# Two queues for the first loads, six cast buffers, and two row tiles transposed in float16

## The chip, the cores and the metric

The kernel runs on one core of a Trainium2 chip. The time is in device microseconds (us) for one execution of the whole program. Before the change three runs took 305.96, 309.68 and 311.07 us, so the median is 309.68. The run that was profiled took 306.58 us, and its profile spans 304.8 us from the first to the last instruction.

The engines have short names in the profile: PE is TensorE (matmuls; PEld are its weight loads), DVE is VectorE, ACT is ScalarE, POOL is GpSimd, SP is SyncE. Each works through its own instructions in order. A letter q behind a name (SPq) means the sequencer of that engine, which issues DMAs.

## The reference

```python
def setup_inputs():
    batch, m, k, n = 16, 512, 1024, 768
    return {
        "x": np.random.randn(batch, m, k).astype(np.float32),
        "w1": np.random.randn(k, n).astype(np.float32),
        "w2": np.random.randn(k, n).astype(np.float32),
    }

def reference(x: np.ndarray, w1: np.ndarray, w2: np.ndarray) -> np.ndarray:
    y1 = np.matmul(x, w1)
    y2 = np.matmul(x, w2)
    return (np.tanh(y1) * y2).astype(np.float32)
```

All inputs and the output are float32. There are 16 x 512 = 8192 rows of x with 1024 columns, and two weights of 1024 x 768.

## The kernel before

**Tiling.** The rows of x are cut into 64 row tiles of 128 rows (`mt`, 0 to 63). The contraction of 1024 is cut into eight slices of 128 (`k`). A weight slice a0 to a7 is 128 rows of w1, b0 to b7 of w2. The 768 output columns are cut into 512 (`F`) and 256 (`G`). All products are float16 with float32 sums. TensorE needs x with its contraction on the partitions, so every row tile is transposed first; the result is called `xT`.

**Three stages.** The first six row tiles, the head, are multiplied plainly: eight slices for each output, at L434. Row tiles 6 to 62 are 19 triples. For a triple, a fast matrix multiplication scheme is used: sums of x blocks (`S`, on VectorE, L419) are multiplied with sums of weight blocks (`B`, L409) in 15 products of four matmuls with 512 columns each (L462), and the products are combined with copies on ScalarE (L468) and additions on VectorE (L477). In this way 60 matmuls do the work of 72. Row tile 63 is plain again. Each output tile is a tanh on ScalarE (L440, L480) and a multiplication on VectorE (L444, L485), and is then stored by SyncE (L428).

**How x and the weights come in.** In the head, SyncE alone loads float32 data: row tiles 0 to 3 (`x0` to `x3`, 512 KB each, L332, into tiles called `x_f`) and the 16 weight slices (384 KB each, L336, into `w_f`), in the order of the list `loads` (L520): x0 a0 x1 a1 x2 a2 x3 a3 a4 and so on up to b7. Twelve buffers hold weight slices, so the last four wait until a slice has been cast to float16 (`cast_w`, L344; the copy itself is L340 on ScalarE or L342 on VectorE). Row tiles 0 to 3 are transposed on TensorE in float32, in two halves of four 128x128 blocks each (`transpose_pe`, L349), and each half is copied from PSUM to `xT` as float16 (`evacuate`).

From row tile 4 on, GpSimd issues a DMA that casts to float16 while loading (`load_x`, L369, into `xh`). Row tiles 4 and 5 are transposed on TensorE in float16 (`transpose_pe_h`, L359; eight blocks go into one bank). All later ones are transposed by a DMA that SyncE issues (L372).

**Buffers.** The cast tiles `xh` of row tiles 6 and up rotate through three buffers. Row tiles 4 and 5 have two buffers of their own, which are then not used again. A load into a buffer (`load_x`) waits until the transpose of the row tile that used it has landed (`T`), and until ScalarE has summed that tile's absolute values (`D`, L375). That sum, taken for every row tile and weight slice, feeds a test at the end of the kernel: if a magnitude is out of range, a slower general path would run. `xT` has four sets of three buffers.

**What sets the order.** A planner in the file (`Planner`, L78) simulates all operations with costs and due times, and its result is the order in which instructions are emitted on each engine, and the choice between ScalarE and VectorE where both are possible. It models DMA as one stream: `bandwidth` (L138) is the time at which the stream is free, `xfer` a transfer's length and `latency` the time to landing. The order of the products in a triple is written by hand (`PE_ORDER`, L75). While the first loads run, TensorE performs `WARM` matmuls of 256 columns on constant data (L724); nothing uses their results.

Of the kernel before, what the change touches and what calls it, by code (L numbers as in the profile page):

```python
# [77 lines left out]
class Planner:  # L78
# [13 lines left out]
    def op(self, name, engines, due, needs, fn, *args, behind=(), issued=(), chains=(), xfer=0.0, latency=None, seeds=False):  # L92


        assert name not in self.ops, name
        self.ops[name] = dict(engines=engines, due=due, needs=[n for n in needs if n], behind=[n for n in behind if n], issued=[n for n in issued if n], fn=fn, args=args,
                              chains=chains, xfer=xfer, latency=latency, seeds=seeds)
        for c in chains:
            self.chains.setdefault(c, {"left": 0, "bank": None, "end": 0.0})["left"] += 1
# [35 lines left out]
    def run(self, soon):  # L135
        free = {"none": 0.0, "pe": 0.0, "act": 0.0, "dve": 0.0, "pool": 0.0, "sp": 0.0}
        port = {"dve": 0.0, "pool": 0.0}
        bandwidth = 1.75  # L138
        left = {n: len(o["needs"] + o["behind"] + o["issued"]) for n, o in self.ops.items()}
        ready_at, end, engine_of, start_of = dict.fromkeys(self.ops, 0.0), {}, {}, {}  # L140
        ready = {e: [] for e in free}
# [10 lines left out]
        while len(end) < len(self.ops):  # L152
            best = None
            for e, names in ready.items():
# [20 lines left out]
                s, due, n = min((o for o in options if o[0] <= first + 0.02), key=lambda o: o[1])  # L175
                ahead = max(0.4, self.LOOK * self.ops[n]["engines"][e])
                urgent = [o for o in options if o[0] < first + ahead and o[1] + lag < min(due + lag, o[0] + 1.0)]
                if urgent and e != "pe":
                    s, due, n = min(urgent, key=lambda o: o[1])
# [6 lines left out]
            s, e, n = best  # L186
# [8 lines left out]
            f = s + o["engines"][e]  # L195
# [3 lines left out]
            if o["xfer"]:  # L199
                bandwidth = max(bandwidth, f) + o["xfer"]  # L200
# [32 lines left out]
def kernel(  # L233
# [17 lines left out]
    nc = tc.nc  # L251
    P = 128
    B, M, K = x.shape
    _, N = w1.shape
    KO = K // P
    KH = KO // 2
    MT = B * M // P
# [3 lines left out]
    TAIL = 1  # L261
    TRIPLES = (MT - HEAD - TAIL) // 3
    LOW, HIGH = 512.0, 1024.0
    XH_BUFS, XT_BUFS, S_BUFS, O_BUFS, C_BUFS, WF_BUFS = 3, 4, 2, 3, 2, 12
    WARM = 12
    SOON = {"S": 3.0, "D": 3.0}
    STORED = 5
    GATE = 2
    POOL_FROM = 99
    BY_PE = 6  # L270
    FILL = (-10, -6, -4, -2)
    bf16, f16, f32, i32 = mybir.dt.bfloat16, mybir.dt.float16, mybir.dt.float32, mybir.dt.int32

    xf = x.flatten_outer_dims().rearrange("(mt p) k -> mt p k", p=P)
# [8 lines left out]
    xhpool = pool("xh", 1)  # L283
# [16 lines left out]

    head_stack = ExitStack()
    wfpool = head_stack.enter_context(tc.tile_pool(name="wf", bufs=WF_BUFS))
    xfpool = head_stack.enter_context(tc.tile_pool(name="xf", bufs=4))
    steady = {}

    pin = tc.keep_in_program_order
# [1 line left out]
    plan = Planner(8)  # L308
    op = plan.op
# [6 lines left out]
    xfs, wfs, xhs, xts, ss, cs, os_ = {}, {}, {}, {}, {}, {}, {}  # L316
# [3 lines left out]
    def home(pool, key, shape, dtype):  # L320

        if (pool.name, key) not in fixed:
            fixed[pool.name, key] = pool.tile(shape, dtype, name=key)
        return fixed[pool.name, key]
# [3 lines left out]
        return xts[mt]  # L328

    def load_xf(e, mt):  # L330
        xfs[mt] = xfpool.tile([P, K], f32, tag="xf", name="x_f")
        pin(nc.sync.dma_start(xfs[mt], xf[mt]))  # L332

    def load_w(e, t, k, queue):
# [3 lines left out]
    def copy(e, dst, src):  # L338
        if e == "act":
            pin(nc.scalar.copy(dst, src))  # L340
        else:
            pin(engine[e].tensor_copy(dst, src))  # L342

    def cast_w(e, t, k):  # L344
        copy(e, wh[:, k, t * N:(t + 1) * N], wfs[t, k])

    def transpose_pe(e, mt, h, chain):
        for k in range(KH):
# [12 lines left out]
    def evacuate_h(e, mt, chain):  # L361
        copy(e, x_t(mt).rearrange("p k m -> p (k m)"), bank(chain).bitcast(f16))

    def xh_slot(mt):
        return XH_BUFS + mt - 4 if mt < BY_PE else (mt - BY_PE) % XH_BUFS

    def load_x(e, mt):
        xhs[mt] = home(xhpool, f"xh{xh_slot(mt)}", [P, K], f16)
        pin(nc.gpsimd.dma_start(xhs[mt], xf[mt]))  # L369

    def transpose(e, mt):
# [148 lines left out]
    plan.strict = [f"{p}.{i}" for _, i, p in sorted(sequence)]  # L520

    loads = "x0 a0 x1 a1 x2 a2 x3 a3 a4 a5 a6 a7 b0 b1 b2 b3 b4 b5 b6 b7".split()
    slices = [("ab"[t], t, k) for t in range(2) for k in range(KO)]
    for n, what in enumerate(loads):
        i = int(what[1])
        xfer = 1.3 if what[0] == "x" else 1.02
        before = f"L{loads[n - 1]}" if n else ""
        if what[0] == "x":
            op(f"L{what}", {"sp": 0.05}, 0.1 * n - 100, [], load_xf, i, issued=[before], xfer=xfer, latency=0.6)
        else:  # L530
            t = "ab".index(what[0])
            j = t * KO + i - WF_BUFS
            op(f"L{what}", {"sp": 0.05}, 0.1 * n - 100, [], load_w, t, i, nc.sync,
               issued=[before], behind=[f"c{slices[j][0]}{slices[j][2]}" if j >= 0 else ""], xfer=xfer, latency=0.6)
    for a, t, k in slices:
        op(f"c{a}{k}", {"dve": 0.5, "act": 0.74}, 6 + 1.3 * k + 9.5 * t,
           [f"L{a}{k}"], cast_w, t, k)
        op(f"aw{a}{k}", {"act": 0.92}, 80 + 10 * (t * KO + k), [f"c{a}{k}"], abs_w, t, k)
    for mt in range(4):
        for h in range(2):  # L540
            due = 5 + 2.3 * mt + 0.1 * h
            op(f"PT{mt}{h}", {"pe": 0.45}, due, [f"Lx{mt}"], transpose_pe, mt, h, ("T", mt, h), chains=[("T", mt, h)])
            op(f"e{mt}{h}", {"dve": 0.6, "act": 0.5}, due + 0.5, [f"PT{mt}{h}"] + ([f"e{mt}0"] if h else []), evacuate, mt, h,
               ("T", mt, h), chains=[("T", mt, h)])
        op(f"D{mt}", {"act": 1.05}, 30 + mt, [f"PT{mt}1"], abs_x, mt)

    PRODUCERS = {mt: [f"e{mt}0", f"e{mt}1"] if mt < 4 else [f"T{mt}"] for mt in range(MT)}
    xt_readers = {mt: [] for mt in range(MT)}

    def plain(mt, t, which, chain, due, at=0, first=True, behind=()):  # L550
        for k in range(KO):
            needs = ([f"cb{k}"] if t or which == "M" else []) + ([f"ca{k}"] if not t or which == "M" else [])
            needs.append(f"e{mt}{k // KH}" if mt < 4 else f"T{mt}")
            if not first and k == 0:
                needs.append(f"m{mt - 1}{t}{which}0")
            before = list(behind) + ([f"m{mt}{t}{which}0"] if k else [])
            n = G if which == "G" else F
            rhs = wh[:, k, t * N + (F if n == G else 0):t * N + F + (G if n == G else 0)]
            if which == "M":
                rhs = wh[:, k, :].rearrange("p (t n) -> p t n", t=2)[:, :, F:]  # L560
            op(f"m{mt}{t}{which}{k}", {"pe": MG if n == G else MM}, due(k), needs, mm, chain, slice(at, at + n), mt, k,
               rhs, first and k == 0, behind=before, chains=[chain])
        last = [f"m{mt}{t}{which}{k}" for k in range(KO)]
        xt_readers[mt] += last
        return last
# [25 lines left out]
    for mt in list(range(4, HEAD)) + list(range(MT - TAIL, MT)):  # L591
# [6 lines left out]
        for n, (t, which) in enumerate(parts):  # L598
            last = plain(mt, t, which, (which, mt, t), lambda k: base + 1.7 * n + 0.2 * k,
                         behind=[plan.strict[FILL[n]]] if tail else ())  # L600
# [23 lines left out]
    for v, a, b, how in B_SUMS:  # L624
        needs = []
# [22 lines left out]
    for i in range(TRIPLES):  # L648
        for v, a, b, how in A_SUMS:
            op(f"S{v}.{i}", {"pool": 1.12} if v in ON_POOL and i >= POOL_FROM else {"dve": 0.34}, None, x_needs(i, a) + x_needs(i, b), x_sum, i, v, a, b, how,  # L650
               behind=[f"{r}.{i - S_BUFS}" for r in a_readers[v]] if i >= S_BUFS else [])
# [3 lines left out]
        for o in C_OPS:  # L655
            name, kind, needs = o[:3]
            needs = [f"{n}.{i}" for n in needs]
            chains = sorted({(i, p) for p in o[3:6] if isinstance(p, str) and p[0] == "c"})
# [9 lines left out]
            if kind in ("seed", "copy", "add"):  # L668
                before = []
                if o[3][0] == "s":  # L670
                    before = [f"{r}.{i - C_BUFS}" for r in readers[o[3]]] if i >= C_BUFS else ["pools"]
# [6 lines left out]
            mt = HEAD + 3 * i + r  # L678
            due = soonest[name] + LAST + slot_of[i, "p10"]
            if kind in ("t", "th"):  # L680
                lo, n = (0, F) if kind == "t" else (F, G)
                op(f"{name}.{i}", {"act": 0.5 if n == F else 0.29}, due, needs, c_tanh, i, r, o[4], lo, n, o[5],
                   behind=reuse_out(mt), chains=chains)
            else:
                lo, n, at = (0, F, 0) if kind == "m" else (F, G, G)
# [9 lines left out]
    for mt in range(MT - TAIL - 3):  # L695
        op(f"st{mt}", {"sp": 0.05}, 40 + 4.33 * mt if mt >= HEAD else 110 + 13 * mt, outs[mt], store, mt,
           issued=[f"T{HEAD + 3 * (STORED + mt)}"] if mt < HEAD else [], xfer=1.1)
    for mt in range(4, MT):
        j = mt - XH_BUFS
        prev = f"L{mt - 1}" if mt > 4 else "gate"  # L700
        op(f"L{mt}", {"pool": 0.55}, None, [], load_x, mt,
           issued=[prev], behind=[f"T{j}", f"D{j}"] if j >= BY_PE else [], xfer=1.5)
        if mt < BY_PE:
            op(f"PT{mt}", {"pe": 0.5}, None, [f"L{mt}"], transpose_pe_h, mt, ("T", mt), chains=[("T", mt)])
            op(f"T{mt}", {"dve": 0.67, "act": 0.93}, None, [f"PT{mt}"], evacuate_h, mt, ("T", mt), chains=[("T", mt)])
            plan.ops[f"PT{mt}"]["due"] = 26 + 4 * (mt - 4)
        else:
            op(f"T{mt}", {"sp": 1.35}, None, [f"L{mt}"], transpose, mt,
               issued=[f"T{mt - 1}"] if mt > BY_PE else [],
               behind=xt_readers[mt - 3 * XT_BUFS] if mt >= 3 * XT_BUFS else [], xfer=1.45, latency=2.2)  # L710
        op(f"D{mt}", {"act": 1.05}, ORIGIN - 12 + 4.33 * (mt - HEAD), [f"L{mt}"], abs_x, mt)
# [8 lines left out]
    order = plan.run(SOON)  # L720
# [3 lines left out]
        pin(nc.tensor.matmul(banks[n % 8][:, n // 8 % 2 * 2 * P:][:, :2 * P], ones.bitcast(bf16)[:, :P], ones.bitcast(bf16), start=True, stop=True))  # L724
    make_identity(nc, ident)
    pin(nc.vector.tensor_copy(ident_h, ident))
    for n in sorted(order, key=lambda n: plan.start_of[n]):
        o = plan.ops[n]
        o["fn"](plan.engine_of[n], *o["args"])
    fast.close()  # L730
# [100 lines left out]
```

## Time and profile before

| | us |
|---|---|
| median of three runs (lowest, highest) | 309.68 (305.96, 311.07) |
| profiled run; span of its profile | 306.58; 304.8 |
| TensorE busy | 294.0 (96%) |
| VectorE busy | 239.8 (79%) |
| ScalarE busy | 221.2 (73%) |
| GpSimd busy | 33.0 (11%) |

The profile has several views, and the prediction uses these. The page gives busy times and 40 slices of the span; in the rows of slices each digit is a share in tenths, and PEclk is the clock that TensorE was granted. A table by stage gives the busy time of PE, PEld, DVE, ACT and POOL in a stretch, with the number of instructions in brackets, then the granted clock, the share of time in which the 16 DMA engines had a packet in work, and GB/s. The timeline lists instructions by start and length; in square brackets stands how long the engine was idle before, and which engine and tile ended that. The list of waits adds these up: engine, line, what it waited for, us in total, times, longest. Matmuls are pipelined, and the length drawn for one (0.379 us for 512 columns) is longer than the distance from one start to the next; a gap of TensorE is therefore longer than it looks.

### The profile page before, as it was taken

The page shows a single profiled execution, that of the slowest core. Times are in us where ns is not written, and L with a number is a line of the kernel's source. Part 1 is how long each engine was busy: PE and PEld are TensorE (multiplying, and loading weights), DVE is VectorE, ACT ScalarE, POOL GpSimd, SP SyncE. Part 2 cuts the span into 40 slices and gives each one's busy share as a digit, 9 for nine tenths or more (in the row PEclk, how much of TensorE's full clock was granted, in tenths as well). Part 3 has the DMA queues.
Part 4 walks back from the last instruction along what each step waited for, and adds up shares of the span by engine and source line. Part 5 has one row for each costly group of instructions (what it writes and reads, how often), then busy time and mean ns, then how long its engine had stood idle before and what let it go on. Part 6 is the DMA issues. An engine that isn't in the chain of part 4 may idle for free. (4 is left out here: it accounts for less than half of the span.)

```text
span 304.8 us, 4455 instructions
## 1 busy us (share of the span) xinstructions
PE 294.0 (96%) x1409; PEld 138.7 (45%) x1409; DVE 239.8 (79%) x497; ACT 221.2 (73%) x438; POOL 33.0 (11%) x67
## 2 busy tenths in 40 slices
PE   6999999999999799999999999999999999999994
PEld 4665544444444344444444444444444444444442
DVE  1217999888969597878988889797978989789754
ACT  4598978989885758687586866858686777775641
POOL 0030111110201011011020201111011101100000
PEclk9799999999999999999999999999999999999999
DMA  7999989999999999999999999999999999992143
GB/s 242 412 399 219 163 135 133 149 157 280 169 204 281 162 262 242 211 257 243 253 219 235 243 207 187 235 212 205 251 187 208 178 239 226 170 260 103 69 175 123
DMA packets 82585, 64.80 MB, mean 213 GB/s; under 512 B 63616, under 2 KB 64128, under 8 KB 82560
## 3 DMA queue, kind: packets, MB, share of 16 engines
q1 hardware_dynamic: 73920, 48.77, 66.0%
q0 software_dynamic: 8640, 15.73, 34.6%
q8 instruction: 11, 0.18, 0.2%
q14 instruction: 14, 0.11, 0.2%
HBM read 39.85 MB, written 25.17 MB: 213 GB/s over the span
## 5 line engine op out<-in xcount | busy, mean ns | idle before, releaser
L462 PE MATMUL bank<-b,s 128*128 128x512 f16 x608 | 141.0, 379 | 0.3 <-DVE bank L477 0.3
L462 PEld LDWEIGHTS <-s 128*128 128x128 f16 x760 | 74.4, 98 | 90.1 <-issue 0.6
L477 DVE TENSOR_TENSOR bank<-bank,s 128x512 f32<-128x512 f32 x95 | 65.8, 694 | 27.0 <-ACT s L468 17.6
L468 ACT ACTIVATE s<-bank 128x512 f32<-128x512 f32 x95 | 55.7, 594 | 42.3 <-PE bank L462 42.3
L375 ACT ACTIVATE junk<-xh 128x1024 f16<-128x1024 f16 x60 | 63.0, 1050 | 0.2
L485 DVE TENSOR_TENSOR o<-o,bank 128x256 f32<-128x256 f32 (+1 forms) x114 | 60.6, 546 | 1.4 <-ACT o L480 1.0
L462 PEld LDWEIGHTS <-xT 128*128 128x128 f16 x380 | 36.7, 98 | 49.2 <-issue 6.1
L462 PE MATMUL bank<-b,xT 128*128 128x512 f16 x228 | 55.4, 379 | 0.0
L369 POOL DMA_DIRECT2D xh<-in_x_dram x60 | 32.1, 537 | 213.2 <-ACT junk L375 82.4
L462 PE MATMUL bank<-wh,xT 128*128 128x512 f16 x152 | 39.0, 379 | 3.1 <-ACT o L480 2.9
L480 ACT ACTIVATE o<-bank 128x256 f32<-128x256 f32 x76 | 31.7, 435 | 12.5 <-DVE bank L477 7.5
L434 PE MATMUL bank<-wh,xT 128*128 128x512 f16 (+1 forms) x208 | 39.5, 344 | 0.4 <-ACT xT L340 0.4
L462 PE MATMUL bank<-wh,s 128*128 128x512 f16 x152 | 39.0, 379 | 0.0
L419 DVE TENSOR_TENSOR s<-s,xT 128x512 f16<-128x512 f16 x76 | 31.5, 416 | 1.2 <-DMA xT<-xh 1.1
L480 ACT ACTIVATE o<-s 128x512 f32<-128x512 f32 x38 | 23.9, 628 | 10.5 <-DVE s L477 10.4
L434 PEld LDWEIGHTS <-xT 128*128 128x128 f16 x208 | 20.2, 99 | 17.5 <-ACT xT L340 1.4
L468 ACT ACTIVATE bank<-bank 128x512 f32<-128x512 f32 x38 | 20.4, 568 | 2.7 <-PE bank L462 2.4
L419 DVE TENSOR_TENSOR s<-xT,xT 128x512 f16<-128x512 f16 x38 | 15.8, 418 | 3.9 <-DMA xT<-xh 3.8
L342 DVE CAST wh<-w_f 128x768 f16<-128x768 f32 x7 | 3.9, 560 | 17.6 <-DMA w_f<-in_w_dram 17.6
L477 DVE TENSOR_TENSOR bank<-s,bank 128x512 f32<-128x512 f32 x19 | 13.2, 692 | 5.3 <-PE bank L462 4.3
L419 DVE TENSOR_TENSOR s<-xT,s 128x512 f16<-128x512 f16 x38 | 15.8, 415 | 0.0
L375 ACT ACTIVATE junk<-wh 128x768 f16<-128x768 f16 x16 | 13.5, 843 | 0.2
(40 smaller groups left out, 121.4 us busy)
## 6 DMA issues: line engine op xcount, KB each, us to landing
out_dram<-o SPq DMA_DIRECT2D x60, 384.0 KB, 5.1
xh<-in_x_dram POOLq DMA_DIRECT2D x60, 256.0 KB, 5.6
w_f<-in_w_dram SPq DMA_DIRECT2D x16, 384.0 KB, 8.3
x_f<-in_x_dram SPq DMA_DIRECT2D x4, 512.0 KB, 7.0
out_dram<-o SPq DMA_DIRECT2D x4, 256.0 KB, 2.3
xT<-xh SPq DMA_TRANSPOSE x58, 5.8
out_dram<-o SPq DMA_DIRECT2D x4, 128.0 KB, 1.9
```

Of the source, the lines that this page charges most:

```text
L342: pin(engine[e].tensor_copy(dst, src))
L369: pin(nc.gpsimd.dma_start(xhs[mt], xf[mt]))
L375: pin(nc.scalar.activation(junk[:, :src.shape[-1]], src, ACT.Abs, scale=scale, accum_out=sums[:, column:column + 1]))
L419: pin(engine[e].tensor_tensor(ss[i, v], x_operand(i, a), x_operand(i, b), OP[how]))
L434: pin(nc.tensor.matmul(b, xts[mt][:, k, :], rhs, start=first, stop=k == KO - 1, skip_group_check=True))
L462: pin(nc.tensor.matmul(place(i, dst), x_operand(i, a)[:, k, :], w_rhs(b, k), start=begins and k == 0, stop=k == KH - 1, skip_group_check=T ...
L468: pin(nc.scalar.activation(d, place(i, src), ACT.Copy, scale=float(sign)))
L477: pin(nc.vector.tensor_tensor(d, a, b, ALU.add if signs == (1, 1) else ALU.subtract))
L480: pin(nc.scalar.activation(out_tile(HEAD + 3 * i + r)[:, lo:lo + n], place(i, src)[:, :n], ACT.Tanh, scale=float(sign)))
L485: pin(nc.vector.tensor_tensor(o, o, place(i, src)[:, at:at + n], ALU.mult))
```

## The change

Four things change together.

1. The first four weight slices are issued by ScalarE's queue, ahead of all other work there. SyncE's queue keeps x0 to x3 and the remaining slices. The purpose is that x and weights come in side by side.
2. Row tiles 2 and 3 (`WIDE` = 2 and up) are cast to float16 by VectorE or ScalarE after the load (`cast_x`), transposed on TensorE in float16 as row tiles 4 and 5 are, and evacuated in one piece of 1024 columns instead of two of 512.
3. The cast buffers of the later row tiles grow from three to six. Three rotate at first; at row tiles 18, 24 and 30 one more joins. The first two of these are the buffers that row tiles 4 and 5 had; the third is new.
4. The warm-up has 21 matmuls instead of 12, and the planner's model of the first loads is adapted: the stream starts at 1.6 instead of 1.75, a weight slice takes 0.98 instead of 1.02, and a load from SyncE has the general latency of 1.6 instead of 0.6.

```diff
-        bandwidth = 1.75
+        bandwidth = 1.6
...
-    XH_BUFS, XT_BUFS, S_BUFS, O_BUFS, C_BUFS, WF_BUFS = 3, 4, 2, 3, 2, 12
-    WARM = 12
+    XT_BUFS, S_BUFS, O_BUFS, C_BUFS, WF_BUFS = 4, 2, 3, 2, 12
+    WARM = 21
...
+    WIDE = 2
+    XH_FEW, XH_MORE = 3, (18, 24, 30)
...
+    def cast_x(e, mt):
+        xhs[mt] = home(xfpool, f"xh{mt}", [P, K], f16)
+        copy(e, xhs[mt], xfs[mt])
+
...
-    def xh_slot(mt):
-        return XH_BUFS + mt - 4 if mt < BY_PE else (mt - BY_PE) % XH_BUFS
+    xh_slot, xh_user, turn = {}, {}, []
+    for mt in range(4, MT):
+        if mt < BY_PE:
+            xh_slot[mt], xh_user[mt] = XH_FEW + mt - 4, None
+        elif mt < BY_PE + XH_FEW:
+            turn.append((mt - BY_PE, None))
+        elif mt in XH_MORE:
+            slot = XH_FEW + XH_MORE.index(mt)
+            turn.insert(0, (slot, slot - XH_FEW + 4 if slot - XH_FEW + 4 < BY_PE else None))
+        if mt >= BY_PE:
+            xh_slot[mt], xh_user[mt] = turn.pop(0) if mt >= BY_PE + XH_FEW else turn[-1]
...
+    early = ("a0", "a1", "a2", "a3")
...
-            op(f"L{what}", {"sp": 0.05}, 0.1 * n - 100, [], load_xf, i, issued=[before], xfer=xfer, latency=0.6)
+            op(f"L{what}", {"sp": 0.05}, 0.1 * n - 100, [], load_xf, i, issued=[before], xfer=xfer)
...
-            op(f"L{what}", {"sp": 0.05}, 0.1 * n - 100, [], load_w, t, i, nc.sync,
-               issued=[before], behind=[f"c{slices[j][0]}{slices[j][2]}" if j >= 0 else ""], xfer=xfer, latency=0.6)
+            op(f"L{what}", {"sp": 0.05}, 0.1 * n - 100, [], load_w, t, i, nc.scalar if what in early else nc.sync,
+               issued=[before], behind=[f"c{slices[j][0]}{slices[j][2]}" if j >= 0 else ""], xfer=xfer)
...
-    for mt in range(4):
+    for mt in range(WIDE, 4):
+        due = 5 + 2.3 * mt
+        op(f"X{mt}", {"dve": 0.67, "act": 0.93}, due, [f"Lx{mt}"], cast_x, mt)
+        op(f"PT{mt}", {"pe": 0.5}, due, [f"X{mt}"], transpose_pe_h, mt, ("T", mt), chains=[("T", mt)])
+        op(f"T{mt}", {"dve": 0.67, "act": 0.93}, due + 0.5, [f"PT{mt}"], evacuate_h, mt, ("T", mt), chains=[("T", mt)])
+        op(f"D{mt}", {"act": 1.05}, 30 + mt, [f"X{mt}"], abs_x, mt)
+    for mt in range(WIDE):
...
-        j = mt - XH_BUFS
+        j = xh_user[mt]
...
-           issued=[prev], behind=[f"T{j}", f"D{j}"] if j >= BY_PE else [], xfer=1.5)
+           issued=[prev], behind=[f"D{j}"] + [f"{u}{j}" for u in ("T", "PT") if f"{u}{j}" in plan.ops] if j else [], xfer=1.5)
...
-    for n in sorted(order, key=lambda n: plan.start_of[n]):
+    for n in sorted(order, key=lambda n: (n[1:] not in early or n[0] != "L", plan.start_of[n])):
```

More of the change, by code (lines that the diff above doesn't have):

```diff
@@ L302 @@
     wfpool = head_stack.enter_context(tc.tile_pool(name="wf", bufs=WF_BUFS))
-    xfpool = head_stack.enter_context(tc.tile_pool(name="xf", bufs=4))
+    xfpool = head_stack.enter_context(tc.tile_pool(name="xf", bufs=1))
     steady = {}
@@ L330, in load_xf @@
     def load_xf(e, mt):
-        xfs[mt] = xfpool.tile([P, K], f32, tag="xf", name="x_f")
+        xfs[mt] = home(xfpool, f"xf{mt}", [P, K], f32)
         pin(nc.sync.dma_start(xfs[mt], xf[mt]))
@@ L362, in evacuate_h @@
         copy(e, x_t(mt).rearrange("p k m -> p (k m)"), bank(chain).bitcast(f16))
-    def xh_slot(mt):
-        return XH_BUFS + mt - 4 if mt < BY_PE else (mt - BY_PE) % XH_BUFS
+    xh_slot, xh_user, turn = {}, {}, []
[9 more added lines that the diff above has]
+            xh_slot[mt], xh_user[mt] = turn.pop(0) if mt >= BY_PE + XH_FEW else turn[-1]
+            if mt < BY_PE + XH_FEW:
+                turn[-1] = mt - BY_PE, mt
+            else:
+                turn.append((xh_slot[mt], mt))
     def load_x(e, mt):
-        xhs[mt] = home(xhpool, f"xh{xh_slot(mt)}", [P, K], f16)
+        xhs[mt] = home(xhpool, f"xh{xh_slot[mt]}", [P, K], f16)
         pin(nc.gpsimd.dma_start(xhs[mt], xf[mt]))
@@ L525 @@
         i = int(what[1])
-        xfer = 1.3 if what[0] == "x" else 1.02
+        xfer = 1.3 if what[0] == "x" else 0.98
         before = f"L{loads[n - 1]}" if n else ""
         if what[0] == "x":
-            op(f"L{what}", {"sp": 0.05}, 0.1 * n - 100, [], load_xf, i, issued=[before], xfer=xfer, latency=0.6)
+            op(f"L{what}", {"sp": 0.05}, 0.1 * n - 100, [], load_xf, i, issued=[before], xfer=xfer)
         else:
@@ L545 @@
         op(f"D{mt}", {"act": 1.05}, 30 + mt, [f"PT{mt}1"], abs_x, mt)
-    PRODUCERS = {mt: [f"e{mt}0", f"e{mt}1"] if mt < 4 else [f"T{mt}"] for mt in range(MT)}
+    PRODUCERS = {mt: [f"e{mt}0", f"e{mt}1"] if mt < WIDE else [f"T{mt}"] for mt in range(MT)}
     xt_readers = {mt: [] for mt in range(MT)}
@@ L552, in plain @@
             needs = ([f"cb{k}"] if t or which == "M" else []) + ([f"ca{k}"] if not t or which == "M" else [])
-            needs.append(f"e{mt}{k // KH}" if mt < 4 else f"T{mt}")
+            needs.append(f"e{mt}{k // KH}" if mt < WIDE else f"T{mt}")
             if not first and k == 0:
```

## The prediction

> **What bounds the kernel now.** I read the page first: who is busy, and when.
>
> ```profile
> span 304.8 us, 4455 instructions
> PE 294.0 (96%) x1409; PEld 138.7 (45%) x1409; DVE 239.8 (79%) x497; ACT 221.2 (73%) x438; POOL 33.0 (11%) x67
> PE   6999999999999799999999999999999999999994
> PEclk9799999999999999999999999999999999999999
> ```
>
> TensorE sets the time. The slices show where it isn't full: the first, the twelfth to fourteenth, the last; the clock dips once, in the second. In the order of starts, matmuls of 512 columns follow each other every 0.216 us (14 of them take 3.19 us, of which the last one's drawn length is 0.379: 2.81/13). The 19 triples hold 60 each: 1140 x 0.216 = 246 us, which nothing in this change touches. So I need the idle time of TensorE, by stage. The stage table (us, PE busy, PEld, DVE, ACT, POOL, then clock, DMA share, GB/s) and the same cut finer for the start:
>
> ```profile
> 10.00:15.00 5.00, 4.76 (x28) 3.28 (x27) 1.12 (x2) 2.92 (x7) 0.00 (x0) 0.80 1.03 412
> 15.00:20.00 5.00, 5.00 (x34) 3.02 (x33) 0.69 (x1) 4.82 (x7) 0.00 (x0) 1.00 1.03 402
> 80.00:100.00 20.00, 19.56 (x91) 8.71 (x90) 17.18 (x37) 14.09 (x28) 2.12 (x4) 1.00 1.24 230
> 100.00:150.00 50.00, 48.16 (x223) 21.55 (x222) 40.67 (x89) 36.54 (x73) 5.83 (x11) 1.00 1.10 236
> 150.00:200.00 50.00, 49.77 (x232) 22.43 (x230) 43.27 (x93) 36.79 (x73) 6.36 (x12) 1.00 1.13 220
> ```
>
> ```profile
> 4.50:5.00 0.50, 0.50 (x4) 0.50 (x3) 0.00 (x0) 0.00 (x0) 0.00 (x0) 1.00 0.74 117
> 9.00:10.00 1.00, 1.00 (x5) 0.44 (x4) 0.56 (x1) 0.73 (x2) 0.00 (x0) 0.50 1.03 415
> ```
>
> From 13 us to 80 us TensorE is practically never idle. Before that it waits for loads, and from 8.6 to 12 us it runs at half clock. From 80 us on it loses 3.4 us in the stage table; each gap also hides some 0.16 us of a drawn matmul tail, and counted by starts, from 41 us to the end, eight gaps lose 4.7 us (0.6 near 91, 1.96 near 105, 0.4 each near 198, 211 and 224, the rest smaller).
>
> Next the timeline of TensorE at the start, for the loads:
>
> ```profile
> 4.14 1.55 PE L349 MATMUL bank<-ident,x_f 128*128 128x128 f32 x8 [0.33 <-DMA x_f<-in_x_dram]
> 5.90 0.50 PE L434 MATMUL bank<-wh,xT 128*128 128x512 f16 x2 [0.21 <-ACT xT L340]
> 8.05 1.51 PE L349 MATMUL bank<-ident,x_f 128*128 128x128 f32 x8 [1.65 <-DMA x_f<-in_x_dram]
> 14.55 1.04 PE L349 MATMUL bank<-ident,x_f 128*128 128x128 f32 x8
> ```
>
> Row tile 0 is there at 4.1, its first weight slice at 5.2 (a cast on VectorE waits for it until 5.19), row tile 1 at 8.0, the second slice at 9.0. Then the timeline around the largest gap:
>
> ```profile
> 101.78 1.24 SPq L372 DMA_TRANSPOSE xT<-xh  x1
> 104.91 0.42 DVE L419 TENSOR_TENSOR s<-xT,xT 128x512 f16<-128x512 f16 x1 [1.47 <-DMA xT<-xh]
> 106.50 0.38 ACT L480 ACTIVATE o<-bank 128x256 f32<-128x256 f32 x1 [1.59 <-DVE bank L477]
> 106.93 1.02 PE L462 MATMUL bank<-wh,xT 128*128 128x512 f16 x4 [1.80 <-ACT o L480]
> ```
>
> Read downward it is one chain: a transpose issued 3 us before it was needed, VectorE waiting 1.47 for it, ScalarE's tanh waiting for VectorE, TensorE waiting for the bank that tanh empties. Why was it late? Two lists of waits answer (us in all, times, longest):
>
> ```profile
> POOL xh L369 <- ACT junk L375: 82.4, 24, 6.9
> POOL xh L369 <- DMA xT<-xh: 43.9, 9, 10.5
> SPq L372 <- DMA xh<-in_x_dram: 71.2, 33, 11.2
> ```
>
> The cast load waits for its buffer (freed by the absolute sum on ScalarE and by the transpose), the transpose waits for the load. The load takes 5.6 us to land and the transpose 5.8 (medians of the page): 11.4 us of a buffer's life, before the absolute sum and queueing, against 3 x 4.3 = 13 us that three buffers give at 13 us a triple. The ring has 1.6 us of slack.
>
> **What the skill says.** "DMA: Bandwidth & Descriptors", Issuing engines are not separate DMA queues: loads from two engines run on the same 16 DMA engines, and a second issuer saves issue time only. The trace agrees that issue is cheap: SyncE's first loads go out every 0.45 us, while 512 KB at 0.4 MB/us takes 1.3. The same page, Queues, rings and completion order: each engine alternates between queues packet by packet. Before 20 us this trace has one queue, so it can't show that. "TensorE: Matmul & The Clock Gate", Part 1: half clock until a window of about 3.4 us has been busy, half clock again after an idle one. The trace agrees: 0.21 us a transpose up to 5.2, 0.11 after, half clock for 3.4 us from 8.6 on.
>
> **The change, part by part.**
>
> *Two queues.* ScalarE issues a0 to a3 before anything else: 4 x 0.43 us. With its table load of 1.28 that ends by 0.75 + 1.7 + 1.3 = 3.8; its first copy began at 5.26, so this is free, whichever comes first. SyncE issues x0 to x3. If queues alternate packet by packet, rows of 4096 and 3072 bytes take turns, and x_i and a_i land together when the pair used to be complete: 5.1, 9.0, 11.2, 13.4. The weights gain nothing, and x0 to x3 lose about 1 us each. If they share by bytes, the shorter slices run ahead: x1 would be whole after 2.05 MB instead of 1.41, x2 after 3.07 instead of 2.30, which at 0.4 MB/us is 1.6 and 1.9 us. On the good side, DMA moved 117 to 270 GB/s from 4.5 to 6 instead of 380; over 4.0 to 6.5 that is 0.65 MB instead of 0.95, 0.8 us. Two queues may close that dip or not; I credit 0.3.
>
> *Nine more warm-up matmuls*, at (2.74 - 0.4)/11 = 0.213: 1.9 us. The block ends at 1.07 + 21 x 0.213 = 5.55. Queued behind it are row tile 0's transposes, and for those wait its evacuations and the first products. With x0 landing at 5.1 that costs 0.4; the transposes then run at full clock (0.9 instead of 1.55). The first product moves from 5.9 to about 6.7. That alone costs nothing: the next pair isn't there until 9.
>
> *Row tiles 2 and 3 in float16.* Eight float32 transposes took 1.39 (11.3 us, partly half clock) and 1.04 us; eight float16 ones take 0.61 in the trace (at 30.3). Saved on TensorE: 0.78 + 0.43 = 1.2 us, in a stretch where it is nearly full. Added: two casts 128x1024, 0.69 to 0.75 on VectorE by the 0.56 of 128x768, or about 1.05 on ScalarE; four evacuations of 0.59 to 0.69 become two of 0.69. That is 0.1 to 0.7 us more for two engines that are busy 1.1 and 2.9 of these 5 us: hidden. The new wait (load, cast, transpose) delays tiles 2 and 3 by 0.7 each; products of tiles 0 and 1 are queued meanwhile.
>
> *Sum for the head:* +1.2, +0.3, less about 0.8 for x1 arriving at 8.9 instead of 8.0: 0.7 us gained. Lower bound -1 (x tiles late by bytes), upper +3 (the half clock from 8.6 gone: up to half of 3.4 us; the dip gone; the float16 gain).
>
> *Buffers.* A fourth joins at tile 18, a fifth at 24, a sixth at 30 (their loads stood near 67, 93 and 118 us). From there the ring has 17, 22, 26 us for its 11.4. The gaps near 91 and 105 come from late transposes and lie behind tile 18: 2.56 us by starts. The other 2.1 us aren't transposes (near 198, 211 and 224 tanh is late behind a busy VectorE); I leave them. Gain 2.4, bounds 0 and 4.
>
> *Between runs.* The median, 309.68, is 3.1 us above the profiled run's 306.58. If that is more of the same lateness, buffers take some away; the trace can't tell. I take 1.3, bounds 0 and 3.
>
> The planner's new load times shift its order; TensorE's order within the triples is fixed by hand, so I cost that at nothing, with its risk in the last rival.
>
> Forecast: 309.7 - 0.7 - 2.4 - 1.3 = 305.3 us.
>
> **The rivals.**
>
> *Head pays fully too.* Loads come sooner, the clock stays up, the gaps of late transposes go and the median falls to the best run. For: the dip and the half clock are real. Against: one product pair (0.33 us) is all that the first loads release. 309.7 - 2.5 - 3.5 - 2.7 = 301.
>
> *Nothing arrives.* The DMA engines are taken for more than their whole time (share 1.10 to 1.24 from 60 to 250), so loads that start earlier only lengthen transposes and stores; and the x tiles' later landing eats the float16 gain. For: those shares. Against: 200 to 236 GB/s there, but 412 in the head. 309.
>
> *Slower.* Loads run ahead in bursts and push transposes from 5.8 to 8 us and more, or the re-planned queues put a waiting instruction ahead of an urgent one. A loss like that near 198 (0.4 us) once in each of 19 triples is 8 us: 317. For: VectorE is busy 85% and works in order. Against: more buffers only add freedom, and transposes wait for loads today.
>
> **How the numbers follow.** Forecast 0.50, head pays too 0.30, nothing arrives 0.13, slower 0.07. Two per cent is 6.2 us: faster means below 303.5, slower above 315.9. The second case is faster, and a little of the forecast's edge: 0.33. Slower 0.07, within 0.60. The range goes from 300.5 (second case, nearly whole) to 310 (third case with its noise).
>
> **What would show it.** First product near 6.7; x1 and a1 landing together near 9; float16 transposes of tiles 2 and 3 at 0.6 us a tile; triples starting near 40.4 instead of 41.1; no wait of VectorE for a transpose over 0.5 us behind 80 us; GpSimd's waits shorter after tile 18, and transposes seldom waiting for a load. The prediction is wrong if the clock stays up through 12 us (faster), if new TensorE gaps appear behind 60 us (slower), or if the spread between runs has another cause than late transposes.

## The result and the profile after

The changed kernel takes 317.79 us (median of 4 runs, 315.67 to 319.32); beside it the kernel before took 307.82 (304.93 to 311.07, 4 runs). The ratio is 1.040, with a 95% interval of 1.027 to 1.053: slower by 4%. The forecast was 305.3, between 300.5 and 310. Here and below medians and ranges are of all runs, while a ratio compares only the undisturbed runs of both kernels, those within 1.5% of each kernel's fastest, and so isn't the quotient of the medians.

The page of the changed kernel, the same rows as were shown of before:

```profile
span 317.3 us, 4477 instructions
PE 296.2 (93%) x1418; PEld 138.0 (43%) x1418; DVE 238.8 (75%) x496; ACT 223.1 (70%) x439; POOL 32.7 (10%) x67
PE   7899999999999695998999796899999999999995
PEclk9999999999999998999999999999999999999999
```

The clock no longer dips in the second slice. But between the fourteenth and the twenty-sixth slice, 103 to 206 us, TensorE has holes. The stage table of the changed kernel (us, busy time of PE, PEld, DVE, ACT, POOL, clock, DMA share, GB/s):

```profile
4.50:5.00 0.50, 0.50 (x6) 0.39 (x4) 0.00 (x0) 0.00 (x0) 0.00 (x0) 1.00 1.02 408
9.00:10.00 1.00, 0.88 (x6) 0.35 (x4) 0.00 (x0) 0.54 (x2) 0.00 (x0) 1.00 1.02 409
10.00:15.00 5.00, 3.98 (x33) 2.52 (x34) 1.39 (x2) 4.78 (x6) 0.00 (x0) 1.00 1.03 404
100.00:150.00 50.00, 42.39 (x186) 18.13 (x184) 33.52 (x72) 29.19 (x58) 5.30 (x10) 0.97 1.21 202
150.00:200.00 50.00, 45.32 (x208) 20.09 (x207) 38.90 (x83) 33.77 (x70) 5.29 (x10) 1.00 1.20 203
```

The start is better: 408 GB/s where there were 117, the full clock from 9 to 10 us where there was half. Then 100 to 200 us: TensorE was busy 97.9 of 100 us before and is busy 87.7 now. Counted from one start to the next, gaps and slow stretches behind 20 us cost 18.6 us, against 4.7 before. That is 13.9 us lost, and about 1 us gained at the start; the span of the profiled run is 12.5 us longer.

TensorE's timeline at the start of the changed kernel:

```profile
5.30 1.06 PE L355 MATMUL bank<-ident,xf 128*128 128x128 f32 x8
6.61 0.50 PE L453 MATMUL bank<-wh,xT 128*128 128x512 f16 x2 [0.24 <-ACT xT L342]
7.40 1.09 PE L355 MATMUL bank<-ident,xf 128*128 128x128 f32 x8 [0.29 <-DMA xf<-in_x_dram]
10.72 0.62 PE L365 MATMUL bank<-ident_h,xh 128*128 128x128 f16 x8 [0.84 <-ACT xh L342]
```

Row tile 1 is there at 7.4 (8.0 before), its weight slice at 7.9 (9.0). The first product of a triple starts at 38.4 instead of 41.1, the sixtieth at 56.5 instead of 57.5; head work is still mixed in there, so the second number is the fairer one.

The largest gap, in the timeline of all engines of the changed kernel:

```profile
109.28 3.78 SPq L391 DMA_TRANSPOSE xT<-xh  x1
121.42 0.43 DVE L438 TENSOR_TENSOR s<-xT,xT 128x512 f16<-128x512 f16 x1 [4.97 <-DMA xT<-xh]
123.74 0.39 ACT L499 ACTIVATE o<-bank 128x256 f32<-128x256 f32 x1 [3.55 <-DVE bank L496]
123.86 0.48 PE L481 MATMUL bank<-wh,xT 128*128 128x512 f16 x1 [3.69 <-DVE bank L496]
```

It is the same chain as in the gap at 105 us before: transpose, VectorE, ScalarE, TensorE. The transpose was issued in good time, 12.1 us before VectorE could go on; it took all of that to land. Counted by starts TensorE's gap is 3.85 us, and it is followed by half clock from 124.0 to 127.4, which costs 1.7 us more. The lists of waits of the changed kernel:

```profile
POOL xh L388 <- ACT junk L394: 88.0, 24, 5.9
POOL xh L388 <- DMA xT<-xh: 73.1, 15, 11.0
DVE s L438 <- DMA xT<-xh: 22.4, 11, 5.0
```

```profile
SPq L391 <- PE bank L481: 70.7, 33, 5.6
SPq L391 <- DMA xh<-in_x_dram: 32.5, 12, 11.8
```

Transposes wait less for their load (32.5 us instead of 71.2), which was the purpose, and longer for TensorE to leave an `xT` buffer (70.7 instead of 31.7). VectorE waits more for transposes all the same: 22.4 us instead of 4.9. What lies between is how long a DMA takes from issue to landing. From 100 to 200 us, first before, then in the changed kernel (count, KB, median us):

```profile
out_dram<-o SPq DMA_DIRECT2D x28, 384.0 KB, 5.0
xh<-in_x_dram POOLq DMA_DIRECT2D x23, 256.0 KB, 5.2
xT<-xh SPq DMA_TRANSPOSE x23, 5.8
```

```profile
out_dram<-o SPq DMA_DIRECT2D x24, 384.0 KB, 9.1
xh<-in_x_dram POOLq DMA_DIRECT2D x20, 256.0 KB, 9.6
xT<-xh SPq DMA_TRANSPOSE x20, 10.8
```

Every kind of transfer takes nearly twice as long, though fewer of them were moved. For a transpose, more than half of the added time passes before its first packet: from issue to there the median is 5.7 us instead of 3.1, from first to last packet 3.7 instead of 2.2. Stores and transposes of SyncE share a queue, called q1 in the profile, so a transpose also waits for what SyncE issued before it.

### The profile page after: what moved, and what is told of

Same layout as the page of the kernel before. It is cut to its first block, busy times and chain, and to the rows that moved or that the text cites. A ratio compares the mean times of both kernels' runs of the same rounds, so it can differ in the third digit from the quotient of the medians.

```text
span 317.3 us, 4477 instructions
## 1 busy us (share of the span) xinstructions
PE 296.2 (93%) x1418; PEld 138.0 (43%) x1418; DVE 238.8 (75%) x496; ACT 223.1 (70%) x439; POOL 32.7 (10%) x67
## 5 line engine op out<-in xcount | busy, mean ns | idle before, releaser
L481 PE MATMUL bank<-b,xT 128*128 128x512 f16 x228 | 56.3, 383 | 0.1
L481 PE MATMUL bank<-wh,xT 128*128 128x512 f16 x152 | 39.7, 384 | 8.7 <-DVE bank L496 5.0
L438 DVE TENSOR_TENSOR s<-xT,s 128x512 f16<-128x512 f16 x38 | 15.8, 415 | 0.0
L344 DVE CAST wh<-w_f 128x768 f16<-128x768 f32 x5 | 2.8, 560 | 14.5 <-DMA w_f<-in_w_dram 14.5
```

Source lines behind the costliest of these rows:

```text
L438: pin(engine[e].tensor_tensor(ss[i, v], x_operand(i, a), x_operand(i, b), OP[how]))
L481: pin(nc.tensor.matmul(place(i, dst), x_operand(i, a)[:, k, :], w_rhs(b, k), start=begins and k == 0, stop=k == KH - 1, skip_group_check=T ...
```

## The experiments

**Theory A**: the cast buffers do the harm. More loads in flight crowd the DMA engines, and transposes land late. **Theory B**: the head's changes, or the new plan that the planner makes of any change, do it. Times are medians with the range of the runs. The kernel before ran beside each group, and took 309.14 us (23 runs, 304.93 to 316.58), 309.95 (23), 309.02 (23) and 313.5 (7 runs, 304.07 to 318.14); it scatters by 4%, which limits what single medians tell. Where no interval is given, the runs scattered too widely for one. A kernel has four runs unless another number is given, and its interval then rests on two to four of them.

**Three buffers again, in the changed kernel** (`after_three_bufs`)

```diff
-    XH_FEW, XH_MORE = 3, (18, 24, 30)
+    XH_FEW, XH_MORE = 3, ()
```

> The changed kernel with three cast buffers again (all of the head's changes stay; planned anew). Theory A, the buffers do the harm (loads that run ahead crowd the transposes): the gaps between 100 and 210 us go, head gain stays, about 303 to 306 us. Theory B, the new plan or the head does it: it stays at 314 or more.

Measured: 311.08 us (304.33 to 314.19, 4 runs). Most of the loss is gone, but the time lies between the two expectations, and 303 to 306 came only once. The scatter is that of the kernel before.

**Six buffers in the kernel before** (`before_six_bufs`): the changed kernel's `xh_slot`, `xh_user` and the wait of `load_x`, and nothing else.

> The kernel before with six cast buffers, planned anew; head untouched. Theory A: slower than before by some 10 to 14 us, about 320 (no head gain to set against it). Theory B (the head's changes and their new plan): about 306 to 309.

Measured: 318.15 us (315.11 to 326.71), ratio 1.035 (1.020 to 1.051). The buffers, with the order planned for them, bring the loss without the head's changes. Theory B falls for the head.

**Six buffers, old order** (`before_six_bufs_old_order`): buffers as above, but the planner is told of three.

```diff
-        j = mt - XH_BUFS
+        j = mt - 3
```

> The kernel before with six cast buffers, but planned as if there were three: the instructions of every engine keep the order of before, only the loads may start earlier. If early loads crowd the transposes on the DMA engines: 314 or more. If the harm is the order that the planner makes of six buffers (two transposes in a row, then two stores): 303 to 308, the same as before or a little faster.

Measured: 314.03 us (310.0 to 316.6), ratio 1.027 (1.017 to 1.037, from two runs). By the tiles' names in the traces the order is as before but for one pair of instructions each on VectorE and ScalarE, so earlier loads alone cost time. How much is less sure. The profiled run is the fastest one, 310.0; in it transposes land in 6.8 us from 100 to 200 us, against 11.1 with six buffers and the order planned for them, and VectorE waits 8.1 us for them in all, against 16.5. With six buffers the planner more often puts two transposes and then two stores in a row on SyncE, and that may add to the harm. The two intervals overlap, so the order's share is not shown.

**Only the planner's numbers** (`before_new_times`): `bandwidth` 1.6, `xfer` 0.98, no own latency.

> The kernel before with only the planner's three numbers for the first loads changed (1.6, 0.98, general latency). A control for what planning anew does by itself: within 2% of before, 304 to 311; if planning anew is itself the cause, 314 or more.

Measured: 310.26 us (305.27 to 326.31, 20 runs), ratio 1.002 (0.997 to 1.008). This new plan changes nothing by itself.

**Four and five buffers** (`after_four_bufs`, `after_five_bufs`, `before_four_bufs`): `XH_MORE` is (18,) or (18, 24).

> The changed kernel with a fourth cast buffer from row tile 18 on and no more (three buffers gave 311.1, six 317.8). If the harm grows with the number of loads that may be in flight: between the two, 312 to 316. If it is a matter of the last buffers, or of the plan alone: 311 or 318.

> The changed kernel with cast buffers four and five (from row tiles 18 and 24), without the sixth. Four gave 306.5, six 317.8. If each further load in flight adds crowding: 309 to 315.

> The kernel before with a fourth cast buffer from row tile 18, planned anew. If the gain of the changed kernel with four buffers came from the buffer: 305 to 308 here. If it came from the head: 309 to 311, as before.

Measured: with the changed head, four buffers 306.47 us (302.29 to 309.39), five 319.20 (314.28 to 323.43), ratio 1.029 (1.012 to 1.047). With the old head, four buffers 305.13 us (302.36 to 314.53, 20 runs), ratio 0.992 (0.989 to 0.996). So the harm doesn't grow buffer by buffer, as I had expected of it: the fourth helps with the old head, the fifth tips it over. With four buffers the two heads can't be told apart in this scatter. The kernel before with one more buffer beats the kernel before by 0.8%, and so the changed one. Its page has no hole in TensorE's row:

```profile
span 301.3 us, 4455 instructions
PE   6899999999999999999999999999999999999994
```

**More room for transposes** (`before_five_xt`, `before_six_bufs_five_xt`): A narrower form of Theory A, called A1, was that a transpose is late because it may only be issued once TensorE has left its `xT` buffer. `XT_BUFS` becomes 5, with three and with six cast buffers.

> The kernel before with three cast buffers and five sets of transposed tiles instead of four. Theory A1 (a transpose is late because it may only be issued when TensorE has left its buffer): SyncE waits less for TensorE, but loads are the limit with three cast buffers, so 305 to 310, as before.

> The kernel before with six cast buffers and five sets of transposed tiles. Theory A1: with 13 us more room a landing time of 11 us instead of 6 no longer matters, so the 318.2 of six buffers falls to 309 or less. Theory A2 (the DMA engines lose throughput when loads and transposes overlap, whatever the room): it stays at 315 or more, and transposes still take 8 us and more to land.

Measured: 309.07 us (306.53 to 318.96, 20 runs), ratio 1.005 (1.000 to 1.009), and 321.77 us (319.15 to 322.88), ratio 1.048 (1.035 to 1.062). A1 falls. The landings of the second kernel, 100 to 200 us:

```profile
xh<-in_x_dram POOLq DMA_DIRECT2D x21, 256.0 KB, 9.5
xT<-xh SPq DMA_TRANSPOSE x22, 11.3
```

**Less traffic** (`after_short_stores`, `before_short_stores`): stores of row tiles 6 to 59 carry only the last 256 columns.

```diff
     def store(e, mt, lo=0, n=N):
+        if HEAD <= mt < MT - TAIL - 3:
+            lo, n = F, G
```

> The changed kernel, but the triples' outputs (row tiles 6 to 59) are stored only in their last 256 columns: a third of the bytes, so the output is not complete. If the DMA engines are crowded in the triples, transposes land in 6 us or less again and the time falls to 302 to 306. If the order of waits on SyncE does it and not the traffic, it stays above 313.

> The kernel before, with the triples' outputs stored only in their last 256 columns (the output is not complete). With DMA relieved, what is left between this and the changed kernel with short stores (301.95) is the head: 302.6 to 303.0 if the head gained the 0.7 to 1.1 us that the traces suggest, 305 or more if the buffers also help when there is room.

Measured: 301.95 us (301.67 to 302.58) for the changed kernel, 303.54 (302.30 to 303.92) for the one before. The second lies between its two expectations. All waits, buffers and orders are as they were; only bytes are gone, and with them 15.8 us of the changed kernel, more than the whole loss. Its transposes land in 6.0 us from 100 to 200 us, where they took 10.8. Most of the scatter goes too: 0.9 and 1.6 us over four runs each, where the four runs of the full kernels spread over 3.7 (changed) and 6.1 (before). So six buffers do no harm once this traffic is gone. Which traffic isn't told apart: a shorter store takes less of the DMA engines, and it also lets the transpose behind it in the same queue start sooner.

**DMA alone and mixed** (`dma_alone_and_mixed`): a kernel of DMAs only.

> No part of the reference is computed: only DMAs, in stages of 8 row tiles each, twice over: cast loads alone, transposes alone, loads with transposes, stores alone, loads with stores, transposes with stores, all three. A2a (the engines only share their time): a mixed stage takes the sum of its parts. A2b (mixing costs throughput): loads with transposes take over 15% more than the sum of the two alone. If instead mixed stages take less than the sum, the engines aren't full with one kind and crowding must be a matter of order.

Measured, first to last packet of eight row tiles: loads alone 11.9 us; transposes alone 11.1; both together 20.9, less than the sum of 23.0; all three kinds 28.5. The second pass agrees within 0.4 us. Stores had no stage to themselves; by difference they are about 1.0 us a tile (sixteen, with eight loads, took 28.1: 28.1 - 11.9 = 16.2). A2b falls: loads with transposes lose no throughput. A row tile needs 1.49 + 1.39 + 1.01 = 3.9 us of all 16 engines, or 3.6 as measured mixed, and a triple gives it 13/3 = 4.3. By this estimate the engines are 82 to 90% taken.

But mixing decides who goes first. The packets of the mixed stage (count, MB, share of 16 engines), from 53 to 60 us, while loads (q0) and transposes (q1) run together, and then from 63 to 68 us, when the loads are done:

```profile
q0 software_dynamic: 710, 1.29, 97.7%
q1 hardware_dynamic: 592, 0.15, 15.6%
```

```profile
q1 hardware_dynamic: 4515, 1.12, 111.6%
```

Together, the two queues send nearly packet for packet, 710 to 592. A packet of a transpose has 256 bytes and takes some 20 ns of an engine (1.116 x 16 x 5000 / 4515); one of a load takes about 154 (0.977 x 16 x 7000 / 710). So the transposes get 592/7 = 85 packets in a us, against 4515/5 = 903 alone. Beside loads that follow each other without a break, transposes crawl at a tenth of their speed. In the kernel a load's packets last only some 3 us, and the slowing is milder (1.5 to 4.0 us, below).

**The loads held back** (`after_six_held`): all six buffers, but from row tile 18 on GpSimd reads one column of `xT` of four tiles before, and so waits for that transpose, ahead of each load. The planner is told of this wait.

```diff
     def load_x(e, mt):
         xhs[mt] = home(xhpool, f"xh{xh_slot[mt]}", [P, K], f16)
+        if mt >= 18:
+            pin(nc.gpsimd.tensor_copy(held_h, xts[mt - 4][:, 0, :1]))
         pin(nc.gpsimd.dma_start(xhs[mt], xf[mt]))
...
```

> The changed kernel with all six cast buffers, but from row tile 18 on GpSimd issues a load only when the transpose of four row tiles before has landed. If loads that run ahead are the cause: 304 to 308, like four buffers. If it is the buffers themselves (their places, the order planned for them): 314 or more.

Measured: 311.15 us (303.33 to 316.91). It lies between the two expectations, and in the profiled run, one of the long ones at 316.9, transposes still took 8.4 us to land from 60 to 250 us (8.9 in the changed kernel). Holding loads by one transpose doesn't restore what four buffers give. Inconclusive.

**The mix beside the engines' work** (`mixed_with_engines`)

> No part of the reference is computed: eight loads with eight transposes, seven times, beside nothing, VectorE in float16, VectorE on PSUM in float32, ScalarE, TensorE, and all of them (with either VectorE form). If only packets compete: 20 to 21 us in every stage, as alone. If work of an engine slows the DMA: the stage with that engine takes 24 us or more.

Measured, in that order: 20.4, 20.7, 21.2, 20.5, 24.9, 21.1 and 23.2 us. TensorE alone gave the longest stage, but with VectorE in float16 and ScalarE beside it the mix took 21.1. Each stage ran once. Inconclusive.

**The parts of the head** (`after_short_stores_f32_transposes`: `WIDE` = 4; `after_short_stores_one_queue`: `early` = ()), both with short stores, where the scatter is small.

> As after_short_stores (the triples' outputs stored only in their last 256 columns), with row tiles 2 and 3 transposed in float32 again. The float16 transposes were costed at 1.2 us of TensorE: 303.1 if that holds, 301.7 to 302.3 if it was hidden.

> As after_short_stores (the triples' outputs stored only in their last 256 columns), with all first loads on SyncE's queue again. The second queue was credited with 0.3 us and charged with 0.8: 301.4 if that holds; 303 or more if the early second queue is what keeps TensorE's clock up through 12 us.

Measured: 301.98 us (301.92 to 302.04) and 303.11 (302.62 to 303.87), against 301.95. The float16 transposes give nothing; the second queue gives 1.2 us. (301.95 is from another group of runs; within this group the kernel with two queues, the first, is 1.1 us faster than the one with one.) 303.11 meets the number expected for the clock, but not its cause: the profile of the last kernel has the full clock through 12 us. Among the nine profiles with one queue five have no half clock at the start, and none of the seven with two has one. In these seven no half-microsecond between 4.5 and 6.5 us is below 358 GB/s. In each of the nine with one queue there is one of 289 or less. The line of the last kernel for 5.5 to 6 us, where the changed one had 408:

```profile
5.50:6.00 0.50, 0.50 (x6) 0.32 (x3) 0.08 (x1) 0.34 (x1) 0.00 (x0) 1.00 0.85 201
```

## Why the prediction was wrong, step by step

**The bound** held: TensorE sets the time, and its largest gaps behind 80 us end with a transpose that lands late. Why it lands late was read wrongly; see the buffers below.

**Two queues.** x and weights landed closely together, as argued, but at 7.4 and 7.9 instead of 9.0. The charge of 0.8 us was wrong, and the credit of 0.3 too small: the dip closed wholly. The term measured +1.2 us where I had put -0.5. That a second issuer saves issue time only, which the prediction took from the Trainium skill, is not what these runs show: here the loads themselves came faster (the last experiment).

**Warm-up.** First product at 6.61, forecast about 6.7.

**Float16 transposes.** 0.62 and 0.61 us a tile, as read from before. But the 1.2 us were counted as saved "in a stretch where it is nearly full", and with faster transposes it isn't: TensorE is busy 3.98 of the 5 us from 10 to 15, and waits 0.84 us for the new cast. Saved on the path: nothing that can be seen, 301.95 against 301.98.

**Sum of the head.** 0.7 forecast. 1.0 us at the sixtieth product; 1.6 us between the two kernels with short stores (which still differ in buffers and ran in different groups). Right in sum by luck, from two wrong terms.

**Buffers.** This is the step that failed, in its reading and in its sum. The reading was "a transpose issued 3 us before it was needed". But the transpose issued at 101.78 took 5.4 us and landed at 107.2. The one that VectorE waited for until 104.91 was issued earlier; its line in the timeline, and its time to landing:

```profile
94.99 2.73 SPq L372 DMA_TRANSPOSE xT<-xh  x1
DMA to landing us min/median/max: 9.9/9.9/9.9
```

The transpose behind the gap near 91 was issued at 80.84 and took 9.1 us. In the median 5.8 us both would have landed before VectorE wanted them. So what made them late was a slow landing, and the sum held just that fixed.

That sum was "From there the ring has 17, 22, 26 us for its 11.4." It gave a longer ring the old landing times. These belong to the old ring. From 100 to 200 us transposes went from 5.8 to 10.8 us and loads from 5.2 to 9.6, so GpSimd's waits for a buffer, which were to get shorter, grew from 126 to 161 us (82.4 + 43.9 before, 88.0 + 73.1 now). The term was a gain of 2.4 us; in the profiled runs 13.9 were lost.

How do more buffers lengthen the landing? Three buffers don't only make a load wait; they also hold it back from running beside a transpose. I counted packets from 60 to 250 us: in the changed kernel 26 of 43 transposes had a load beside them for over half of their time, and took 4.0 us on average from first to last packet; the others took 1.5. Before it was 17 of 43, with five buffers 34 of 41, with four buffers and the old head 18 of 44. This fits the picture of loads that nobody was waiting for and that, on engines 82 to 90% taken, took the turns of transposes that VectorE was waiting for. It isn't shown as the whole cause: the larger part of the added landing time passes before the first packet, the order that the planner makes of six buffers may have a part in that, and the run that held the loads back didn't confirm it.

**Between runs.** Most of the scatter goes with the short stores, so it has to do with DMA traffic, which fits the guess of late transposes. But six buffers brought none of the 1.3 us: the fastest run of the changed kernel took 315.67.

**The rivals.** "Slower" named the mechanism, bursts of loads that push the transposes beyond 8 us. That it also had the size, 317, is luck: it added 0.4 us in each of 19 triples, and the runs show a few gaps of 1 to 3.85 us between 103 and 206 us. I gave it 0.07, because "more buffers only add freedom". And I answered the DMA shares of 1.10 to 1.24 with a comparison of GB/s, 200 to 236 against 412. That comparison is void: transposes alone, with the engines full, move 190 to 224 GB/s.

The Trainium skill's sentence in "DMA: Bandwidth & Descriptors", Queues, rings and completion order, that an engine alternates between queues packet by packet, was in the prediction, and the DMA kernel agrees with it at 710 to 592. I applied it to the first loads only, and not to the cast loads and the transposes, which are also two queues.

**What stays open.** Why the fourth buffer helps and the fifth tips over; why the hold on four tiles before didn't do what four buffers do; and how the loss divides between the earlier loads and the order planned for them.

## What to carry to other kernels

A full buffer ring can also be a brake. When an engine waits for a transfer, find the issue of that very transfer, and see whether it was issued late or landed slowly; putting more transfers in flight can make a slow landing slower, as here. Before loosening it, work out the DMA time of one round from each kind of transfer by itself and compare it with the round: near full, as here, work that starts earlier can take the place of work that is needed sooner. In the DMA kernel the transposes, with packets of 256 bytes, fell from 903 packets in a us to 85 beside loads with packets of 2048. Take landing times from the ring as it is only for that ring, and size it in steps; here one buffer more was worth 0.8% with the old head, and two or three more cost 3 to 4%.

## What was not expected of the hardware

Loads of one queue sag from about 400 GB/s to between 117 and 289 somewhere between 4.5 and 6.5 us, in nine profiles out of nine; loads of the same bytes from two queues stay at 358 or more in seven out of seven. The cause isn't known.

A gap of TensorE of 2 to 4 us in the triples was followed by 3.4 us at half clock in 10 of the 15 cases in the profiles (124.0 to 127.4 us in the changed kernel, eight matmuls that start 0.43 us apart instead of 0.216). That late transpose was paid for nearly one and a half times: 3.85 us and 1.7.
